# Rounds of two and of four experts in turn, one one-hot matrix ahead of the sort, and a branch hint, in a two-layer mixture-of-experts kernel

## The chip, the cores and the metric

The kernel runs on one core of a Trainium2 chip. The metric is device time in microseconds (us) of one launch; for the kernel before, the median of three runs is 997.89 us. Engines are PE (TensorE; PEld is its weight load), DVE (VectorE), ACT (ScalarE), POOL (GpSimd) and SP (SyncE, which here issues the loads of weights).

## The reference

256 tokens of width 1024 go through two layers and then a second block. Each layer is a mixer (a gated recurrence, a latent attention and a spatial gate), and then a sparse feed-forward part; only that part is touched here:

```python
for l in range(2):
    x = x + mixer(rms_norm(x))
    x = x + hier_moe(rms_norm(x))   # 32 experts, every token goes to 2 of them
x = second_block(x)

# hier_moe: the best of 4 groups, then the best 2 of its 8 experts; per expert, over its tokens:
h = silu(xi @ w1[e]) * (xi @ w3[e])   # 1024 -> 256
y = (h @ w2[e]) * weight              # 256 -> 1024
```

In float32 an expert's three matrices are 3 MB, so a layer reads 96 MB of expert weights.

## The kernel before

**Routing.** At the end of the mixer the tokens are scored (`Router`, from line 893). `slot` (line 994) says for each token and expert which place the token has in the expert's list. The eight experts 0 to 7 are static: they stand at places 0 to 7. The other 24 are sorted by the number of their tokens (lines 1000 to 1009, result `idm`) and stand at places 8 to 31; their number is known only then, and SP reads it into a register before it issues such a load (line 219). `perm` and `permb` hold the order as a matrix.

**Rounds.** `experts` works in 11 rounds. Places 0 to 11 go two at a time, with 64 tokens each (rounds 0 to 5, 6 MB of weights a round); places 12 to 31 go four at a time, with 32 tokens each (rounds 6 to 10, 12 MB a round). In either kind the array's 128 columns are full: the experts of a round stand side by side in it. A round does this:

- `onehot` (once for two rounds, on DVE, line 1093) makes the matrix P that picks the round's tokens; `gather` multiplies with it on PE (line 1127) and `gates` does the same for the gate weights (line 1106).
- `hidden` (line 1143) does the first product in two halves, one for each of an expert's first two weight chunks (c0, c1). In the middle of it `mid_way` runs: the second half of `combine` of the round before last, and `turn` of the round before. In round 1 `arrange` also runs there, which puts slots and weights into sorted order.
- `outp` (line 1179) does the second product, with the third chunk (c2), for the round before, and `combine` (line 1193) adds the result to the tokens. The gather for the next pair of rounds is woven into every second `outp`.

**Loads.** Every chunk is one DMA of 1 MB from SP's queue. The list `queue` fixes their order: for each round its c0, then its c1, then c2 of the round before. `pump` issues the next load when a buffer is free; `done` gives a buffer back, in the order of the program. In the expert stage 18 buffers are lent to the list: 5 of `w`, 6 of `a`, 1 each of `b`, `y` and `x`, 2 each of `hi` and `lo`. Loads of the last 8 places may not use `x`, `hi` and `lo` (`LATE`). Three chunks are loaded early, in the mixer, and the next layer's first chunk ("in") stands 8 loads ahead of the end.

**Overflow.** `most`, the highest number of tokens, is read into a register on every engine (line 1060). After the rounds, `tc.If(most > ...)` at line 1268 guards a long body for lists that are too long. With these inputs it is jumped over. `add_x` (line 395) then adds the sums to x on DVE, and the next mixer or the second block begins with transposes of x on PE (line 437).

`warm(n)` (line 386) issues n matmuls on constants, whose result nobody reads. The Tile framework orders the instructions of each engine by its own estimate of times, so instructions of neighbouring steps are interleaved.

Of the kernel before, what the change touches and what calls it, by code (L numbers as in the profile page):

```python
# [24 lines left out]
NE = 32  # L25


STATIC = 8
WIDE = 12
ROUNDS = [(64, list(range(i, i + 2))) for i in range(0, WIDE, 2)] + [(32, list(range(i, i + 4)))  # L30
                                                                    for i in range(WIDE, NE, 4)]
NR = len(ROUNDS)
SLOTS = 64
LATE = 8

N8 = dict(w=5, hi=2, lo=2, h=2, a=6, b=3, y=1, x=1)
N2 = dict(a=2, b=3, c=5)
# [68 lines left out]
def block_kernel(ctx: ExitStack, tc: tile.TileContext, A, out):  # L106
# [45 lines left out]
    def mm(tag):  # L152
        return pp.tile([128, 512], F32, name="mm", tag=f"ps_{tag}", bufs=NPS[tag])
# [10 lines left out]

    def late(key, tag):

        return tag in ("x", "hi", "lo") and key[2] >= NE - LATE

    def pump():

# [44 lines left out]
    def chunk_of(l, e, c):  # L215

        def ap():
            if e not in expert:
                expert[e] = nc.values_load(order[0][0:1, e - STATIC:e - STATIC + 1], engines=[SP], min_val=1,
                                           max_val=NE - STATIC)  # L220
            return A["w_e"][l, bass.ds(expert[e] + (STATIC - 1), 1), c].rearrange("e p n -> p (e n)")
        return (("e", l, e, c), A["w_e"][l, e, c] if e < STATIC else ap)

    for l in range(L):
        ex = []
        for i in range(NR + 1):
            for c in range(2):
                ex.extend(chunk_of(l, e, c) for e in (ROUNDS[i][1] if i < NR else ()))
            ex.extend(chunk_of(l, e, 2) for e in (ROUNDS[i - 1][1] if i else ()))
        for i in range(len(W_IN_CHUNKS)):  # L230
            a, b = W_IN_OFF[i], W_IN_OFF[i + 1]
            if l == 0 or i:
                queue.append((("in", l, i), A["w_in"][l][:, 8 * a:8 * b]))
            if i == 1:
                queue.append((("u", l), A["w_u"][l]))
            if i in EARLY:
                queue.append(ex.pop(0))
        queue.extend((("out", l, i), A["w_out"][l][:, i * 2048:(i + 1) * 2048]) for i in range(4))
        ex.insert(len(ex) - 8, following(l + 1))
        queue.extend(ex)  # L240
# [652 lines left out]
    class Router:  # L893
# [35 lines left out]
        def route(self):  # L929
# [44 lines left out]
            while chains:  # L974
                for c in list(chains):
                    try:
# [16 lines left out]
            slot = t1([128, 2, 32], "slot")  # L993
            nc.vector.scalar_tensor_tensor(slot, pr[:, :64].rearrange("p (j e) -> p j e", j=2), 1.0, ab,
                                           op0=OP.add, op1=OP.mult)

            nd = NE - STATIC
            k0, k1 = t1([128, nd], "key0"), t1([128, nd], "key1")
# [8 lines left out]
            idm = t1([128, nd], "idm", I32)  # L1007
            nc.vector.tensor_copy(idm, sk)
            nc.vector.tensor_scalar(idm, idm, 31, None, op0=OP.bitwise_and)
            perm = t1([NE, NE], "perm")  # L1010
            nc.vector.tensor_copy(perm[:, :STATIC], ident[:NE, :STATIC])
            nc.vector.tensor_scalar(perm[:, STATIC:], idm[:NE], float(STATIC), cc("place")[:NE], op0=OP.add,
                                    op1=OP.is_equal)
            permb = t1([NE, NE], "permb", BF)
            nc.vector.tensor_copy(permb, perm)

            mc, mci = t1([128, 3], "mc"), t1([1, 1], "mci", I32)
            nc.vector.tensor_reduce(mc[:, 0:1], pr[:, 64:64 + STATIC], AX, OP.max)
# [35 lines left out]
            rb_ = bc(rh, 2, NR)  # L1054
            nc.gpsimd.tensor_copy(whl[:, :, :, 0], rb_)
            nc.gpsimd.tensor_tensor(whl[:, :, :, 1], rb_, whl[:, :, :, 0].bitcast(F32), op=OP.subtract)
            weights_of(whl, wg, 0, STATIC)
            order[:] = [idm]
            expert.clear()
            most = nc.values_load(mci[0:1, 0:1], min_val=0, max_val=1 << 14)  # L1060
            lend("hi", N8["hi"])
            lend("lo", N8["lo"])
            lend("x", 1)
            return xh, xl, whl, slot, wg, (perm, permb, k0, sk), most

    def weights_of(whl, w, lo, hi):

        for a, b, n, i in ((lo, min(hi, WIDE), 2, lo // 2), (WIDE, hi, 4, WIDE // 2)):
            if a < b:
                m = (b - a) // n  # L1070
                for j in range(2):
                    v, o = w[:, j, a:b].rearrange("p (i e) -> p i e", e=n), whl[:, j, i:i + m]
                    nc.vector.tensor_copy(o[:, :, 2:2 + 2 * n:2], v)
                    nc.vector.tensor_sub(o[:, :, 3:2 + 2 * n:2], v, o[:, :, 2:2 + 2 * n:2].bitcast(F32))

    def experts(l, xh, xl, whl, slot, wg, perms, most):
# [5 lines left out]
        Ps, gts, hs = {}, {}, {}  # L1082
        X = big("h", [128, 8, 256], name="X")
        yhl = big("h", [128, 2, 2, 512], F32R, name="yhl")

        def onehot(q):

            rounds = ROUNDS[2 * q:2 * q + 2]
            n, places = rounds[0][0], sum((r[1] for r in rounds), [])
            P = Ps[q] = mid("c", [128, 2, 128 * len(rounds)], F32R, name="P")  # L1090
            by = slot if places[-1] < STATIC else slots[0]
            for j in range(2):
                nc.vector.tensor_tensor(P[:, j].rearrange("p (e s) -> p e s", e=len(places)),
                                        bc(cc("iota")[:, :n], 1, len(places)),
                                        bc(by[:, j, places[0]:places[-1] + 1], 2, n), op=OP.is_equal)

        def gates(q):

# [97 lines left out]
        def prepare_four(q, n):  # L1196
            if n:
                gates(q)
            gather(q, (2 * n, 2 * n + 1))

        onehot(0)
        prepare_four(0, 0)
        prepare_four(0, 1)

        slotT = small([NE, 2, 256], BF, name="slotT")
        slots = [None, slotT[:, 0], slotT[:, 1]]
# [5 lines left out]
        def arrange():  # L1212

            pt = mm("a")
            for j in range(2):
                nc.tensor.transpose(pt[:NE, j * 128:(j + 1) * 128], wg[:, j], ident)
            wgT = mid("b", [128, 256], name="wgT")[:NE]
            nc.scalar.activation(wgT, pt[:NE, :256], AF.Copy)
# [8 lines left out]
            nc.scalar.activation(slots[2], ps[:NE, :256], AF.Copy)  # L1227
            ps = mm("a")
            for j in range(2):
                nc.tensor.matmul(ps[:, j * NE:(j + 1) * NE], wgT[:, j * 128:(j + 1) * 128], perm, start=True, stop=True)  # L1230
            weights_of(whl, ps[:, :2 * NE].rearrange("p (j e) -> p j e", j=2), STATIC, NE)

        for i in range(NR):
            q, p = divmod(i, 2)
            last = 2 * q + 2 >= NR
            if i == NR - 2:
                x = big("x", [128, 2, D], name="x")
                for j in range(2):
                    nc.vector.tensor_add(x[:, j], xh[:, j].bitcast(F32), xl[:, j].bitcast(F32))

            def mid_way():
                if i > 1:
                    combine(i - 2, 1)
                if i:
                    turn(i - 1)
                if i == 1:
                    arrange()

            hidden(i, mid_way)
            if i == NR - 1:  # L1250
                reclaim()
                prepare(following(l + 1)[0])
            if p == 0 and not last:
                onehot(q + 1)
            if i:
                outp(i - 1, (lambda n: prepare_four(q + 1, n)) if p and not last else lambda n: None)
        combine(NR - 2, 1)
        turn(NR - 1)
        outp(NR - 1, lambda n: None)
        combine(NR - 1, 1)  # L1260
# [4 lines left out]
    def overflow(l, xh, xl, whl, slot, wg, key, sk, most):  # L1265

        g = vec[l][:, VC["ffn"]:VC["ffn"] + 8]
        with tc.If(most > SLOTS * 32 + 31):

            cap = mid("a", [128, NE], name="cap")  # L1270
            nc.vector.memset(cap, float(SLOTS))
# [410 lines left out]
```

## Time and profile before

| | before |
|---|---|
| median of 3 runs | 997.89 us (997.08 to 1001.84) |
| the profiled execution's own time | 1002.17 us |
| its span | 1000.4 us |
| mean granted TensorE clock | 0.979 |
| PE busy | 946.1 us (95%) |
| DVE, ACT busy | 473.6 us (47%), 378.8 us (38%) |
| DMA, mean | 273 GB/s |

Times in the rows count from the start of the span. The expert stage of the first layer runs from about 150 to 386 us, that of the second from about 532 to 765 us. PE's busy time includes matmuls that stand in the array at the same time, and its ends are modelled, so 95% says little by itself. The granted clock is a share of full speed: 1.00 is 2.4 GHz and 0.50 is 1.2 GHz.

### The profile page before, as it was taken

The page shows a single profiled execution, that of the slowest core. Times are in us where ns is not written, and L with a number is a line of the kernel's source. Part 1 is how long each engine was busy: PE and PEld are TensorE (multiplying, and loading weights), DVE is VectorE, ACT ScalarE, POOL GpSimd, SP SyncE. Part 2 cuts the span into 40 slices and gives each one's busy share as a digit, 9 for nine tenths or more (in the row PEclk, how much of TensorE's full clock was granted, in tenths as well). Part 3 has the DMA queues.
Part 4 walks back from the last instruction along what each step waited for, and adds up shares of the span by engine and source line. Part 5 has one row for each costly group of instructions (what it writes and reads, how often), then busy time and mean ns, then how long its engine had stood idle before and what let it go on. Part 6 is the DMA issues. An engine that isn't in the chain of part 4 may idle for free. (4 is left out here: it accounts for less than half of the span.)

```text
span 1000.4 us, 14950 instructions
## 1 busy us (share of the span) xinstructions
PE 946.1 (95%) x5818; PEld 624.5 (62%) x5820; DVE 473.6 (47%) x1149; ACT 378.8 (38%) x706; POOL 15.9 (2%) x56
## 2 busy tenths in 40 slices
PE   8999999999989887999999999999877999999998
PEld 6888874443433324989884434433323998899996
DVE  5798662221202213688664122212123776787574
ACT  6675532221211113485542221211111555755442
POOL 0100000000000001000000000000000000000000
PEclk9999997999999988999999999999998999999999
DMA  9538484898899996337566898999999443145431
GB/s 357 172 140 326 161 314 189 339 421 347 365 423 405 423 420 261 132 127 276 194 256 230 356 399 349 365 423 401 423 421 373 139 163 126 43 137 201 169 127 42
DMA packets 41438, 273.39 MB, mean 273 GB/s; under 512 B 5128, under 2 KB 7312, under 8 KB 9872
## 3 DMA queue, kind: packets, MB, share of 16 engines
q1 hardware_dynamic: 39008, 268.48, 68.3%
q10 hardware_dynamic: 2352, 3.87, 1.2%
q8 instruction: 49, 0.80, 0.3%
q14 instruction: 29, 0.24, 0.1%
HBM read 271.27 MB, written 2.63 MB: 274 GB/s over the span
## 5 line engine op out<-in xcount | busy, mean ns | idle before, releaser
L1143 PE MATMUL mm<-w,X 128*32 128x512 f32 (+1 forms) x1024 | 189.4, 611 | 8.8 <-DMA w<-in_w_e 8.8
L258 DVE TENSOR_TENSOR wlo<-w,whi 128x1024 fp32r<-128x1024 f32 (+3 forms) x124 | 144.1, 1173 | 29.0 <-ACT whi L257 28.9
L257 ACT ACTIVATE whi<-w 128x1024 fp32r<-128x1024 f32 (+3 forms) x124 | 122.4, 1016 | 75.8 <-issue 42.4
L1179 PE MATMUL mm<-w,ehT 128*32 128x512 f32 (+1 forms) x512 | 140.4, 607 | 4.5 <-DMA w<-in_w_e 2.4
L448 PE MATMUL mm<-hT,whi 128*128 128x256 f32 (+2 forms) x432 | 124.5, 289 | 0.3 <-ACT whi L257 0.3
L450 PE MATMUL mm<-hT,wlo 128*128 128x256 f32 (+2 forms) x432 | 123.8, 287 | 1.1 <-DVE wlo L258 1.1
L449 PE MATMUL mm<-lT,whi 128*128 128x256 f32 (+2 forms) x432 | 123.9, 287 | 0.0
L1143 PEld LDWEIGHTS mm<-w,X 128*32 128x32 f32 (+1 forms) x1024 | 48.3, 121 | 104.8 <-issue 82.9
L449 PE MATMUL mm<-wlo,hT 128*128 128x256 f32 x288 | 83.8, 291 | 1.1 <-DVE wlo L258 1.1
L448 PE MATMUL mm<-whi,hT 128*128 128x256 f32 x288 | 84.7, 294 | 0.0
L450 PE MATMUL mm<-whi,lT 128*128 128x256 f32 x288 | 83.7, 291 | 0.0
L448 PEld LDWEIGHTS mm<-hT,whi 128*128 128x128 f32 (+2 forms) x432 | 80.1, 186 | 2.2 <-ACT whi L257 0.6
L449 PEld LDWEIGHTS mm<-lT,whi 128*128 128x128 f32 (+2 forms) x432 | 80.0, 185 | 1.7 <-issue 1.3
L450 PEld LDWEIGHTS mm<-hT,wlo 128*128 128x128 f32 (+2 forms) x432 | 80.0, 185 | 1.8 <-DVE wlo L258 1.5
L1183 DVE TENSOR_TENSOR yhl<-mm,yhl 128x512 fp32r<-128x512 f32 x44 | 30.4, 691 | 106.6 <-ACT yhl L1182 105.6
L1130 ACT ACTIVATE X<-mm,vec 128x256 f32<-128x256 f32 (+1 forms) x96 | 43.5, 455 | 96.3 <-PE mm L1127 95.3
L1179 PEld LDWEIGHTS mm<-w,ehT 128*32 128x32 f32 (+1 forms) x512 | 32.3, 120 | 70.1 <-issue 53.2
L1151 DVE SCALAR_TENSOR_TENSOR eh<-eh,mm 128x256 f32<-128x256 f32 x22 | 9.3, 421 | 128.1 <-ACT eh L1150 128.1
L1127 PEld LDWEIGHTS mm<-P,xh 128*128 128x128 f32 x192 | 31.1, 200 | 54.7 <-ACT X L1130 34.5
L1150 ACT ACTIVATE eh<-mm,gt 128x256 f32<-128x256 f32 x22 | 10.4, 473 | 128.6 <-PE mm L1143 128.6
L449 PEld LDWEIGHTS mm<-wlo,hT 128*128 128x128 f32 x288 | 55.5, 193 | 2.8 <-DVE wlo L258 1.5
L1168 DVE TENSOR_SCALAR ePT<-mm,C 128x256 fp32r<-128x256 f32 x22 | 10.6, 483 | 97.8 <-ACT ehT L1166 97.8
(460 smaller groups left out, 1487.9 us busy)
## 6 DMA issues: line engine op xcount, KB each, us to landing
w<-in_w_e SPq DMA_DIRECT2D x192, 1024.0 KB, 8.8
w<-in_w_in SPq DMA_DIRECT2D x37, 1024.0 KB, 4.9
w<-in_w_out SPq DMA_DIRECT2D x12, 1024.0 KB, 5.0
w<-in_w_in SPq DMA_DIRECT2D x4, 768.0 KB, 6.1
w<-in_w_up_a SPq DMA_DIRECT2D x2, 1024.0 KB, 4.7
w<-in_w_up_b SPq DMA_DIRECT2D x2, 1024.0 KB, 4.8
w<-in_w_u SPq DMA_DIRECT2D x2, 960.0 KB, 14.7
w<-in_w_in SPq DMA_DIRECT2D x2, 800.0 KB, 8.6
```

What stands on the lines that cost most here:

```text
L257: nc.scalar.activation(hi[:, s_], w[:, s_], AF.Copy)
L258: nc.vector.tensor_sub(lo[:, s_], w[:, s_], hi[:, s_].bitcast(F32))
L448: nc.tensor.matmul(ps, st[0], mv[0], start=first, stop=False)
L449: nc.tensor.matmul(ps, st[0], mv[1], start=False, stop=False)
L450: nc.tensor.matmul(ps, st[1], mv[0], start=False, stop=last)
L1127: nc.tensor.matmul(ps[:, a, :n], t[:, j, k * 128:(k + 1) * 128], P[:, j], start=i == 0, stop=i == 3)
L1130: nc.scalar.activation(X[:, k, :n], ps[:, a, :n], AF.Identity, bias=0.0, scale=g[:, k:k + 1])
L1143: nc.tensor.matmul(ph[w * a:w * a + w], X[:, k, c0:c0 + w], take(kk_[a][k // 4])[:, (k % 4) * 512:(k % 4 + 1) * 512], start=k == 0, stop=k ...
L1150: nc.scalar.activation(h, ph[:, :256], AF.Tanh, scale=gts[q][:, p, 1:2])
L1168: nc.vector.tensor_scalar(PT, pT[:, 256:], cc("place" if w == 64 else "place32"), None, op0=OP.is_equal)
L1179: nc.tensor.matmul(py[w * a:w * a + w], hT[:, c * 128 + w * a:c * 128 + w * a + w], take(kk_[a][2])[:, c * 1024 + n * 512:c * 1024 + (n + ...
L1183: nc.vector.tensor_sub(yhl[:, n, 1], py, yhl[:, n, 0].bitcast(F32))
```

## The change

The order of the rounds becomes 2, 2, 4, 4, 2, 2, 4, 4, 2, 2, 4 experts, by places 0, 2, 12, 16, 4, 6, 20, 24, 8, 10, 28. The loads follow that order with one exception: the first two chunks of round 4 (places 4 and 5, static) come ahead of round 2's. `LATE` becomes the six places of the last two rounds. The first one-hot matrix is built right behind `slot`, ahead of the sort; `perm` and `permb` are built later. `arrange` is cut in two: the places in round 0, the weights in round 1, because round 2 now needs the sorted order. Three warming matmuls stand between the transposes of `slot` and the first gather. `most` is read into the registers just ahead of the last `turn` and no longer in the router, and there a branch hint for PE is set, behind a barrier that keeps the order of instructions and waits for nothing.

```diff
-ROUNDS = [(64, list(range(i, i + 2))) for i in range(0, WIDE, 2)] + [(32, list(range(i, i + 4)))
-                                                                    for i in range(WIDE, NE, 4)]
+ROUNDS = [(64, [a, a + 1]) if a < WIDE else (32, list(range(a, a + 4))) for a in (0, 2, 12, 16, 4, 6, 20, 24, 8, 10, 28)]
 NR = len(ROUNDS)
-LATE = 8
+LOADS = (0, 1, 4, 2, 3, 5, 6, 7, 8, 9, 10)
+LATE = [e for r in ROUNDS[-2:] for e in r[1]]
...
-        return tag in ("x", "hi", "lo") and key[2] >= NE - LATE
+        return tag in ("x", "hi", "lo") and key[2] in LATE
...
-        for i in range(NR + 1):
+        rounds = [ROUNDS[i][1] for i in LOADS]
+        for now, before in zip(rounds + [[]], [[]] + rounds):
             for c in range(2):
-                ex.extend(chunk_of(l, e, c) for e in (ROUNDS[i][1] if i < NR else ()))
-            ex.extend(chunk_of(l, e, 2) for e in (ROUNDS[i - 1][1] if i else ()))
+                ex.extend(chunk_of(l, e, c) for e in now)
+            ex.extend(chunk_of(l, e, 2) for e in before)
...
             nc.vector.scalar_tensor_tensor(slot, pr[:, :64].rearrange("p (j e) -> p j e", j=2), 1.0, ab,
                                            op0=OP.add, op1=OP.mult)
+            P = one_hot(0, slot)
...
-            most = nc.values_load(mci[0:1, 0:1], min_val=0, max_val=1 << 14)
...
-        onehot(0)
-        prepare_four(0, 0)
-        prepare_four(0, 1)
...
         nc.scalar.activation(slots[1], pt[:NE, :256], AF.Copy)
+        warm(3)
+        prepare_four(0, 0)
+        prepare_four(0, 1)
...
-                if i == 1:
-                    arrange()
+                (arrange_places, arrange_weights, lambda: None)[min(i, 2)]()
...
         combine(NR - 2, 1)
+        most = nc.values_load(mci[0:1, 0:1], min_val=0, max_val=1 << 14)
+        tc.no_sync_barrier()
+        tc.mark_branch_hint_location(f"fits{l}", hint=0, engines=[mybir.EngineType.PE])
         turn(NR - 1)
...
-        with tc.If(most > SLOTS * 32 + 31):
+        with tc.If(most > SLOTS * 32 + 31, label=f"fits{l}"):
```

`one_hot` holds the two instructions of the former `onehot`; `arrange_places` and `arrange_weights` hold those of `arrange`, and the weights of a pair of rounds are now split into high and low parts by two instructions for each pair.

## Rows read from the trace of the kernel before

**Rows 1.** The page's second part: GB/s in 40 slices of the span.
```profile
GB/s 357 172 140 326 161 314 189 339 421 347 365 423 405 423 420 261 132 127 276 194 256 230 356 399 349 365 423 401 423 421 373 139 163 126 43 137 201 169 127 42
```
**Rows 2.** First layer by stretch: us; PE, PEld, DVE, ACT, POOL busy; clock, DMA share, GB/s.
```profile
156.00:166.00 10.00, 10.00 (x38) 5.01 (x38) 0.55 (x4) 2.36 (x5) 0.00 (x0) 0.68 0.08 34
166.00:174.00 8.00, 8.00 (x39) 2.59 (x35) 0.90 (x2) 0.47 (x1) 0.00 (x0) 1.00 0.86 335
174.00:190.00 16.00, 16.00 (x73) 7.12 (x71) 4.63 (x18) 5.04 (x11) 0.00 (x0) 1.00 0.98 392
190.00:207.00 17.00, 17.00 (x79) 7.07 (x80) 3.43 (x7) 3.41 (x7) 0.00 (x0) 1.00 0.82 322
...
224.00:241.00 17.00, 17.00 (x78) 6.92 (x78) 3.43 (x7) 3.51 (x8) 0.00 (x0) 1.00 0.80 313
...
258.00:276.00 18.00, 18.00 (x112) 7.05 (x111) 3.59 (x8) 3.76 (x8) 0.00 (x0) 1.00 0.84 343
...
302.00:322.00 20.00, 19.11 (x137) 7.10 (x140) 4.35 (x9) 3.03 (x6) 0.00 (x0) 1.00 1.00 400
...
345.00:382.00 37.00, 32.70 (x160) 9.93 (x159) 8.13 (x11) 5.27 (x10) 0.00 (x0) 0.91 1.01 421
```
**Rows 3.** The same by stretch for the second layer's expert stage.
```profile
523.00:545.00 22.00, 20.07 (x107) 12.32 (x109) 13.12 (x89) 6.33 (x15) 0.99 (x4) 0.92 0.53 194
545.00:569.00 24.00, 24.00 (x109) 9.72 (x105) 5.53 (x20) 5.51 (x12) 0.00 (x0) 1.00 0.97 383
569.00:587.00 18.00, 18.00 (x83) 7.35 (x84) 3.43 (x7) 3.41 (x7) 0.00 (x0) 1.00 0.78 316
...
604.00:621.00 17.00, 17.00 (x80) 6.77 (x81) 3.43 (x7) 3.47 (x7) 0.00 (x0) 1.00 0.80 314
...
638.00:655.00 17.00, 17.00 (x110) 6.73 (x110) 3.43 (x7) 3.47 (x7) 0.00 (x0) 1.00 0.85 343
```
**Rows 4.** Who waited for whom on SP's queue, 140 to 345 us: total, times, longest.
```profile
SPq L1060 <- DVE cf L1042: 6.6, 1, 6.6
```
**Rows 5.** Instructions of PE in order of time: the first products of rounds 2 and 4.
```profile
189.21 0.64 PE L1143 MATMUL mm<-w,X 128*64 128x512 f32 x1
...
223.46 0.64 PE L1143 MATMUL mm<-w,X 128*64 128x512 f32 x1
```
**Rows 6.** Instructions of DVE in order of time, at slots and one-hot matrices, both layers.
```profile
149.98 0.23 DVE L994 SCALAR_TENSOR_TENSOR slot<-mm,ab 128x64 f32<-128x64 f32 x1
...
151.22 0.41 DVE L1093 TENSOR_TENSOR P<-C,slot 128x256 fp32r<-128x256 f32 x1
...
532.01 0.22 DVE L994 SCALAR_TENSOR_TENSOR slot<-mm,ab 128x64 f32<-128x64 f32 x1
```
**Rows 7.** Instructions of PE in order of time: warming, slot's transposes, the first gather.
```profile
144.56 4.98 PE L386 MATMUL mm<-ones_bf 128*128 128x512 bf16 x22
...
150.26 0.39 PE L1209 MATMUL mm<-C,slot 128*32 128x128 f32 x2 [0.32 <-DVE slot L994]
...
151.69 0.50 PE L1127 MATMUL mm<-P,xh 128*128 128x256 f32 x2 [1.03 <-DVE P L1093]
...
152.60 0.58 PE L1127 MATMUL mm<-P,xh 128*128 128x256 f32 x1 [0.42 <-DVE P L1093]
```
**Rows 8.** SP's loads in order of time: the first after the buffers were full, both layers.
```profile
165.80 0.34 SPq L184 DMA_DIRECT2D w<-in_w_e  x1
...
544.83 0.33 SPq L184 DMA_DIRECT2D w<-in_w_e  x1
```
**Rows 9.** All of line 1268 (the branch): min/median/max ns, first and last start.
```profile
L1268 DVEq COMPARE_BRANCH  x2: 63/68/72, 385.4 to 764.2; - x2
...
L1268 PEldq COMPARE_BRANCH  x2: 6202/6220/6239, 386.1 to 765.0; - x2
```
**Rows 10.** Instructions in order of time, DVE and PE, behind the branch.
```profile
386.20 2.48 DVE L395 TENSOR_TENSOR x<-x,mm 128x512 f32<-128x512 f32 x4 [0.71 <-PE mm L1193]
...
392.65 0.66 PE L437 MATMUL mm<-C,x 128*128 128x128 f32 x2 [6.37 <-PEq L1268]
```

More of the change, by code (lines that the diff above doesn't have):

```diff
@@ L29 @@
 WIDE = 12
-ROUNDS = [(64, list(range(i, i + 2))) for i in range(0, WIDE, 2)] + [(32, list(range(i, i + 4)))
-                                                                    for i in range(WIDE, NE, 4)]
+SLOTS = 64
+ROUNDS = [(64, [a, a + 1]) if a < WIDE else (32, list(range(a, a + 4))) for a in (0, 2, 12, 16, 4, 6, 20, 24, 8, 10, 28)]
 NR = len(ROUNDS)
-SLOTS = 64
-LATE = 8
+LOADS = (0, 1, 4, 2, 3, 5, 6, 7, 8, 9, 10)
+LATE = [e for r in ROUNDS[-2:] for e in r[1]]
 N8 = dict(w=5, hi=2, lo=2, h=2, a=6, b=3, y=1, x=1)
@@ L1009, in route @@
             nc.vector.tensor_scalar(idm, idm, 31, None, op0=OP.bitwise_and)
[L1010 to L1015, printed above, removed]
             mc, mci = t1([128, 3], "mc"), t1([1, 1], "mci", I32)
@@ L1056, in route @@
             nc.gpsimd.tensor_tensor(whl[:, :, :, 1], rb_, whl[:, :, :, 0].bitcast(F32), op=OP.subtract)
-            weights_of(whl, wg, 0, STATIC)
+            weights_of(whl, wg, 0)
+            perm = t1([NE, NE], "perm")
+            nc.vector.tensor_copy(perm[:, :STATIC], ident[:NE, :STATIC])
+            nc.vector.tensor_scalar(perm[:, STATIC:], idm[:NE], float(STATIC), cc("place")[:NE], op0=OP.add,
+                                    op1=OP.is_equal)
+            permb = t1([NE, NE], "permb", BF)
+            nc.vector.tensor_copy(permb, perm)
             order[:] = [idm]
             expert.clear()
-            most = nc.values_load(mci[0:1, 0:1], min_val=0, max_val=1 << 14)
             lend("hi", N8["hi"])
@@ L1063, in route, with weights_of, one_hot, experts @@
             lend("x", 1)
[L1064 to L1076, printed above, removed]
+            return xh, xl, whl, slot, wg, (perm, permb, k0, sk), P, mci
+    def weights_of(whl, w, *pairs):
+        for q in pairs:
+            rounds = ROUNDS[2 * q:2 * q + 2]
+            places = sum((r[1] for r in rounds), [])
+            n, m = len(rounds[0][1]), len(rounds)
+            v = w[:, :, places[0]:places[-1] + 1].rearrange("p j (i e) -> p j i e", e=n)
+            o = whl[:, :, 2 * q:2 * q + m]
+            nc.vector.tensor_copy(o[:, :, :, 2:2 + 2 * n:2], v)
+            nc.vector.tensor_sub(o[:, :, :, 3:2 + 2 * n:2], v, o[:, :, :, 2:2 + 2 * n:2].bitcast(F32))
+    def one_hot(q, by):
+        rounds = ROUNDS[2 * q:2 * q + 2]
+        n, places = rounds[0][0], sum((r[1] for r in rounds), [])
+        P = mid("c", [128, 2, 128 * len(rounds)], F32R, name="P")
+        for j in range(2):
+            nc.vector.tensor_tensor(P[:, j].rearrange("p (e s) -> p e s", e=len(places)),
+                                    bc(cc("iota")[:, :n], 1, len(places)),
+                                    bc(by[:, j, places[0]:places[-1] + 1], 2, n), op=OP.is_equal)
+        return P
+    def experts(l, xh, xl, whl, slot, wg, perms, P0, mci):
         nonlocal x
@@ L1081, in experts @@
         po = [[acc() for n in range(2)] for j in range(2)]
-        Ps, gts, hs = {}, {}, {}
+        Ps, gts, hs = {0: P0}, {}, {}
         X = big("h", [128, 8, 256], name="X")
@@ L1086, in onehot @@
         def onehot(q):
[L1088 to L1095, printed above, removed]
+            Ps[q] = one_hot(q, slot if ROUNDS[2 * q][1][0] < STATIC else slots[0])
         def gates(q):
@@ L1210, in experts, with arrange_places @@
         nc.scalar.activation(slots[1], pt[:NE, :256], AF.Copy)
[L1212 to L1218, printed above, removed]
+        warm(3)
+        prepare_four(0, 0)
+        prepare_four(0, 1)
+        def arrange_places():
             ps = mm("a")
@@ L1227, in arrange, with arrange_weights @@
             nc.scalar.activation(slots[2], ps[:NE, :256], AF.Copy)
+        def arrange_weights():
+            pt = mm("a")
+            for j in range(2):
+                nc.tensor.transpose(pt[:NE, j * 128:(j + 1) * 128], wg[:, j], ident)
+            wgT = mid("b", [128, 256], name="wgT")[:NE]
+            nc.scalar.activation(wgT, pt[:NE, :256], AF.Copy)
             ps = mm("a")
@@ L1230, in arrange @@
                 nc.tensor.matmul(ps[:, j * NE:(j + 1) * NE], wgT[:, j * 128:(j + 1) * 128], perm, start=True, stop=True)
-            weights_of(whl, ps[:, :2 * NE].rearrange("p (j e) -> p j e", j=2), STATIC, NE)
+            weights_of(whl, ps[:, :2 * NE].rearrange("p (j e) -> p j e", j=2), *range(1, (NR + 1) // 2))
         for i in range(NR):
```

## Prediction

> **What bounds the kernel now.** I read the page's GB/s slices first. They reach some 420 GB/s in the second half of either expert stage and no more [rows 1], so the question is whether the load queue or an engine sets the end there. The table by stretch answers it. From 345 to 382 us the DMA share is 1.01 at 421 GB/s, and PE is idle for 4 of 37 us; in the first half PE is busy throughout, and the queue runs at 313 to 392 GB/s in the stretches shown [rows 2]. So the first layer's stage goes from PE-bound to queue-bound. The second layer does the same [rows 3].
>
> The size of either limit: a 1 MB chunk at 421 GB/s takes 2.49 us. A round of two needs 6 chunks, 14.9 us of queue; a round of four needs 12, 29.9 us. PE needs 34.25 us from the first product of round 2 to that of round 4, so 17.1 us a round [rows 5]. A round of four has half the tokens per expert but fills the same columns, so I give it the same 17.1 us. Over a layer that is 11 x 17.1 = 188 us of PE against 96 x 2.49 = 239 us of queue. The queue is the limit of the stage as a whole, and what it stands idle is lost unless it is made up for by loads ahead. Only 18 buffers allow that.
>
> So I count the queue's idle time, stretch by stretch, as length x (1 - GB/s / 421). First layer: 1.6 us in 166-174, 1.1 in 174-190, 4.0 in 190-207, 4.4 in 224-241, 3.3 in 258-276, 1.0 in 302-322, together 15.4 [rows 2]. Second layer: 2.2 in 545-569, 4.5 in 569-587, 4.3 in 604-621, 3.2 in 638-655, together 14.2 [rows 3]. Before that comes a longer hole: all 18 buffers are full and the queue stands almost still (34 GB/s in 156-166) until the first round gives a buffer back and SP can issue again, at 165.80 and 544.83 us [rows 2, 8]. That moment is set by PE alone. Everything in a queue-bound stage is counted from it.
>
> **The order of the rounds.** I walk the loads through. The first 18 are in. Until the middle of round 2's first product the releases are as before: c0 and c1 of rounds 0 and 1 and c2 of round 0, ten buffers. Ten loads from 165.8 us end at 190.7, and round 2 starts at 189 and gives back its c0 some 6 us later. So the idle time of 166-207 stays: 6.7 us in the first layer. Then four chunks come back at once, about 195.5, four more after the second half at 200, two from round 1's `outp` at 205: ten loads, booked to 220. PE is at round 3's middle by about 212 and gives back four more. From there each round of four frees 12 buffers, 29.9 us of queue, in 17.1 us of PE: the queue has a free buffer waiting and PE waits for loads instead. Round 4 lies loaded already, so PE passes it and then waits for c2 of round 3. At that point, of the 18 buffers, 4 hold c0 and c1 of round 5, 2 hold c2 of round 4 and 4 are round 3's: ten. Eight are booked, some 20 us of queue. Rounds 4 and 5 then eat 2.2 us of this lead each (17.1 - 14.9), and rounds 6 and 7 build it up again. By this walk the queue does not stand still again.
>
> What goes is then 4.4 + 3.3 + 1.0 = 8.7 us in the first layer, and 4.3 + 3.2 = 7.5 in the second: **16.2 us**. Bounds: nothing, if the lead is eaten up elsewhere, and 15.4 + 14.2 = 29.6 us, if the early holes close as well. I take the walk. The second half of the old stage shows what hides PE's work in a queue-bound stretch: PE's own 17.1 us a round lies under 29.9 us of loads.
>
> **The one-hot matrix ahead of the sort, and the warming.** `slot` ends at 150.21, and the first instruction for P starts at 151.22 only, with the sort's instructions between [rows 6]. The gather starts at 151.69 and waits once more for P before 152.60; these waits are 1.03 and 0.42 us [rows 7]. Right behind `slot` the two instructions of 0.41 us end at about 150.6 and 151.0. The transposes end at 150.65. Three warming matmuls, at 4.98 / 22 = 0.23 us [rows 7], last to 151.33. So the gather starts 0.36 us earlier, and its third matmul some 0.9 us earlier, since P is whole by then: 0.9 us in each layer. Without the warming it would be 1.0 to 1.3, so the warming costs a little unless it holds the clock.
>
> The clock is the larger part. In 156-166 the granted clock is 0.68 in the first layer (6.4 of these 10 us at 1.2 GHz, the rest at 2.4); the second layer shows 0.92 over 523-545 [rows 2, 3]. PE stood idle just ahead, in the waits of [rows 7]. From `slot` to the first load issued again it is 165.80 - 149.98 = 15.8 us in the first layer and 544.83 - 532.01 = 12.8 in the second [rows 6, 8], for the same work: 3.0 us for the longer low clock. With the waits of 1.03 and 0.42 us filled I expect the first layer to be no worse than the second: 3.0 us. Sum: 2 x 0.9 + 3.0 = **4.8 us**. Bounds: a loss of 1.4 (warming for nothing, 2 x 0.7), and 2 x 1.3 + 3.0 + another 3.0 = 8.6, if neither layer loses any clock. It counts in full, because the queue stands still until that first release.
>
> **The branch.** The branch over the unused body takes 6.2 us on PE, 0.07 on DVE [rows 9]. DVE adds x behind it at 386.20 in four steps of 0.6 us; PE's first transposes come at 392.65, released by the branch alone [rows 10]. Without it they need the first step, 386.2 + 0.7 and a little for the signal, 387.1; the other half of the columns for the second pair comes 0.6 later. I take 5.4 us for each layer, **10.8 us**. PE would have time to fetch: behind the hint stands the wait for the last four chunks, 10.0 us of queue against 6.2. Bounds: nothing, and 2 x 6.2 = 12.4 and up to 3 us a layer for the clock behind the gap (the price found above).
> The Trainium skill (Runtime: NRT & Kernel Launch, Instruction fetch mechanics) says that a taken branch whose target lies outside the pages held makes the engine fetch that page first. The 6.2 us agree with it. The same section says that prefetch is purely sequential; by this a hint would fetch nothing, and the sum would lose this term. It is the first rival.
>
> **What I cost at nothing.** The register loads of `most`: SP's wait of 6.6 us for it in the router goes [rows 4], but what was queued behind it were loads into buffers that are full by 156 anyway. At the end they lie under PE's wait for the last chunks. Without that cover they would cost half a microsecond. The sorted places are needed two rounds earlier: SP's 17th and 18th loads now wait for `idm`, while nothing is released until 165.8, and `arrange_places` is three matmuls in round 0. If `idm` were late there, it would be late by the two one-hot instructions, 0.8 us, on queues with 10 us to spare. Two more small DVE instructions for the weights lie under PE. `LATE` opens five buffers to six more chunks, in a queue-bound stretch. The barrier binds the last `turn` behind all of round 9, 0.7 us of PE before loads that come later.
>
> **The sum.** 16.2 + 4.8 + 10.8 = 31.8 us. The profiled execution's span of 1000.4 becomes 968.6 us, its own time 1002.2 becomes 970.4. It was 4.3 us above the median of 997.9; from the median I get **966 us**. A change under 0.5%, 5 us, I count as no change.
>
> **Rivals.**
> - The hint does nothing. For it: nothing in this trace shows what a hint does. Against it: DVE's branch to the same place costs 0.07 us, so a branch is cheap where the target is at hand. 966 + 11 = 977 us. Chance 0.20. The rule of the Trainium skill cited above speaks for this rival.
> - The balance does not come: idle time moves into other stretches, because PE's order of instructions is fixed, and it waits for c2 of round 3 with round 5 loaded behind it. Then 966 + 16 = 982 us. Chance 0.12.
> - Slower: the buffers lock. Round 4's six chunks lie in 6 of the 18 buffers through rounds 2 and 3, and a round of four needs exactly the 12 that are left. If SP cannot run ahead, the queue stands still in each of rounds 2, 3, 6 and 7 while PE works. The gain of 16 us a layer is gone from 4 us of idle a round on; with 8 us a round the sum is 2 x 4 x 8 - 32 = 32 us slower, 1030 us. Against it: releases come chunk by chunk, in the order of the loads. Chance 0.08.
> - More than forecast: the early holes close too or no clock is lost, 945 to 953 us. Chance 0.06.
> - Two of the first failures together, with a small loss from the warming: 993 to 1000 us, no change. Chance 0.04.
>
> My forecast has 0.50. The range takes in the first two rivals and most of the bounds of the three terms: 952 to 986 us. The forecast's own range is 957 to 973. Faster: 0.50 + 0.20 + 0.12 + 0.06 = 0.88; same 0.04; slower 0.08.
>
> **What would show it.** The order: a DMA share of about 1 from round 2's middle to the end of the stage, with PE waiting for loads already in rounds 2 to 5, and the last expert chunk landing some 8 us sooner after the first release. The one-hot: P within 0.5 us of `slot`, the gather without its two waits, and the first release 12 to 13 us after `slot` in both layers. The branch: on PE well under 1 us, transposes 1 to 2 us after the first x is added. I am wrong if the queue shows new holes in rounds 2 and 3, if PE's branch still takes 6 us, or if the clock of the first gather stays low.

## The result, and the profile after

Medians: 968.44 us after (965.36 to 969.91, four runs) against 999.87 us before (997.08 to 1003.12, four runs). The ratio is 0.9684, 95% interval 0.9648 to 0.9719: 31.4 us less. The profiled execution after took 965.36 us with a span of 963.6, the fastest of its four; that of before was slower than its median. So the spans differ by more than the medians do, 36.8 us. Where those went, by stage, with starts read from the two traces (us; first layer, second layer):

| stretch | before | after | less by | forecast |
|---|---|---|---|---|
| `slot` to the first load issued again | 15.81, 12.82 | 10.75, 10.77 | 7.1 | 4.8 |
| that load to the end of the last `combine` | 220.48, 220.47 | 213.06, 212.56 | 15.3 | 16.2 |
| last `combine` to the first transpose of x | 6.37, 6.26 | 0.30, 0.30 | 12.0 | 10.8 |
| from there to the next `slot`, to the end | 139.36, 228.84 | 138.11, 227.93 | 2.2 | bound only |
| start to the first `slot` | 149.98 | 149.80 | 0.2 | 0 |

The load queue first. The GB/s slices of the page after, to be held against [rows 1]:

```profile
GB/s 357 180 131 324 203 249 248 362 417 421 421 421 421 420 417 306 94 171 273 199 251 253 355 416 420 422 420 421 421 420 330 181 159 99 45 175 178 186 118 44
```

The same by stretch, columns as in [rows 2]; the last two lines are of the second layer:

```profile
157.00:166.00 9.00, 9.00 (x47) 3.47 (x45) 1.13 (x4) 1.79 (x5) 0.00 (x0) 1.00 0.87 311
166.00:185.00 19.00, 19.00 (x87) 8.04 (x83) 5.71 (x23) 4.66 (x10) 0.00 (x0) 1.00 1.00 402
185.00:193.00 8.00, 8.00 (x63) 3.73 (x66) 0.36 (x1) 1.74 (x4) 0.00 (x0) 1.00 0.71 262
193.00:210.00 17.00, 15.56 (x100) 4.95 (x96) 3.55 (x8) 2.05 (x4) 0.00 (x0) 1.00 1.00 415
...
246.00:262.00 16.00, 16.00 (x68) 5.23 (x64) 3.46 (x6) 3.12 (x6) 0.00 (x0) 1.00 1.02 421
...
301.00:321.00 20.00, 17.85 (x86) 7.89 (x88) 2.82 (x9) 3.97 (x9) 0.00 (x0) 1.00 1.01 421
...
357.00:374.00 17.00, 16.21 (x103) 6.19 (x96) 5.72 (x10) 4.27 (x8) 0.00 (x0) 1.00 1.01 410
...
547.00:555.00 8.00, 8.00 (x59) 3.71 (x62) 0.13 (x1) 1.74 (x4) 0.00 (x0) 1.00 0.63 242
...
571.00:700.00 129.00, 126.36 (x620) 47.70 (x613) 20.32 (x50) 23.66 (x48) 0.00 (x0) 0.99 1.01 421
```

The dips to 347 and 365 between the slices of 421 are gone. One larger hole is left in each layer behind the first release, 185 to 193 and 547 to 555, and after it the queue runs at its limit to the end. The clock is 1.00 where [rows 2] show 0.68.

DVE and PE in order of time (start, us, engine, line), around `slot` and behind the last round:

```profile
149.80 0.23 DVE L996 SCALAR_TENSOR_TENSOR slot<-mm,ab 128x64 f32<-128x64 f32 x1
...
150.06 0.76 DVE L1085 TENSOR_TENSOR P<-C,slot 128x256 fp32r<-128x256 f32 x2
...
373.03 2.48 DVE L397 TENSOR_TENSOR x<-x,mm 128x512 f32<-128x512 f32 x4 [0.21 <-PE mm L1199]
```

```profile
150.54 0.51 PE L1133 MATMUL mm<-P,xh 128*128 128x256 f32 x2
150.94 0.81 PE L388 MATMUL mm<-ones_bf 128*128 128x512 bf16 x3
151.40 0.47 PE L1133 MATMUL mm<-P,xh 128*128 128x256 f32 x1
...
360.76 3.71 PE L1185 MATMUL mm<-w,ehT 128*64 128x512 f32 x16
364.39 2.30 PE L1199 MATMUL mm<-yhl,ePT 128*128 128x512 f32 x8
366.63 0.43 PE L1165 MATMUL mm<-C,eh 128*128 128x128 f32 x2
366.99 0.29 PE L1169 MATMUL mm<-slotT,bf_ident 32*32 32x256 bf16 x4
367.76 3.64 PE L1185 MATMUL mm<-w,ehT 128*32 128x512 f32 x32 [0.49 <-ACT ehT L1172]
371.33 2.28 PE L1199 MATMUL mm<-yhl,ePT 128*128 128x512 f32 x8
373.91 0.90 PE L439 MATMUL mm<-C,x 128*128 128x128 f32 x4 [0.30 <-DVE x L397]
```

P is built right behind `slot`, and the gather no longer waits for it (two waits in [rows 7]). PE runs the three warming matmuls behind the gather's first two, not ahead of them. PE's transposes begin 0.88 us after DVE's first step at x, where [rows 10] had 6.45, and they now wait for x, not for the branch. Behind the first gap the kernel before ran at the lower clock, the kernel after does not (one line of each, columns as in [rows 2]):

```profile
391.00:398.00 7.00, 5.35 (x24) 5.06 (x25) 3.69 (x7) 5.00 (x15) 3.89 (x16) 0.51 0.04 14
...
374.00:390.00 16.00, 15.68 (x123) 14.60 (x124) 11.52 (x27) 10.64 (x24) 5.71 (x19) 1.00 0.39 136
```

The last `outp`, at 367.76, shows no wait for a load; this is taken up under the experiments.

The branch (columns as in [rows 9]), and SP's first load after the buffers were full (as [rows 8]):

```profile
L1279 PEldq COMPARE_BRANCH  x2: 438/460/481, 372.9 to 734.6; - x2
```
```profile
160.56 0.33 SPq L185 DMA_DIRECT2D w<-in_w_e  x1
...
522.79 0.33 SPq L185 DMA_DIRECT2D w<-in_w_e  x1
```

On PE it falls from 6.22 us to 0.46. The next fence lists who waited for whom on SP's queue from 140 to 345 us. SP's wait for the register load (L1266, the former L1060 of [rows 4]) has not gone: 7.4 us, where it was 6.6. The load now stands behind round 9 in the source, but SP still runs it at 152 us.

```profile
SPq L1266 <- DVE cf L1038: 7.4, 1, 7.4
```

### The profile page after: what moved, and what is told of

It reads as the page before. It is cut to its first block, busy times and chain, and to the rows that moved or that the text cites. A ratio compares the mean times of both kernels' runs of the same rounds, so it can differ in the third digit from the quotient of the medians.

```text
span 963.6 us, 14970 instructions
## 1 busy us (share of the span) xinstructions
PE 937.1 (97%) x5826; PEld 615.8 (64%) x5826; DVE 474.4 (49%) x1149; ACT 377.3 (39%) x706; POOL 15.9 (2%) x56
## 4 chain that ended last, share of the span: by engine, by line
PE 85%; DVE 6%; ACT 5%; DMA 3%; issue 1%; SPq 0%; DVEq 0%; ACTq 0%
PE mm L1149 18%; PE mm L1185 12%; PE mm L450 11%; PE mm L451 11%; PE mm L452 11%; PE mm L1133 6%; PE mm L1199 5%; DMA w<-in_w_e 3%; DVE wlo L260 1%; PE mm L562 1%; ACT whi L259 1%; PE mm L1165 1%; PE mm L567 1%; ACT X L1136 1%; PE mm L680 1%
## 5 line engine op out<-in xcount | busy, mean ns | idle before, releaser
L1185 PE MATMUL mm<-w,ehT 128*32 128x512 f32 (+1 forms) x512 | 134.9, 603 | 1.0 <-ACT ehT L1172 1.0
L1185 PEld LDWEIGHTS mm<-w,ehT 128*32 128x32 f32 (+1 forms) x512 | 31.8, 119 | 66.6 <-issue 59.6
L450 PEld LDWEIGHTS mm<-whi,hT 128*128 128x128 f32 x288 | 55.0, 191 | 1.6 <-issue 0.9
```

What stands on the lines that cost most here:

```text
L450: nc.tensor.matmul(ps, st[0], mv[0], start=first, stop=False)
L1185: nc.tensor.matmul(py[w * a:w * a + w], hT[:, c * 128 + w * a:c * 128 + w * a + w], take(kk_[a][2])[:, c * 1024 + n * 512:c * 1024 + (n + ...
```

## The experiments

Spans hold one execution each, and the first `slot`, ahead of any edit, lies between 149.8 and 154.6 us in them. So the profiles are compared by the first four stretches of the table above, called *release*, *rounds*, *gap* and *mixer* in that order.

**The parts by themselves.** Three kernels hold one part each. The order of rounds and loads alone is the changed kernel less these lines, with P and `perm` built where they were and the register load of `most` back in the router:

```diff
-            P = one_hot(0, slot)
...
-        warm(3)
...
-        tc.no_sync_barrier()
-        tc.mark_branch_hint_location(f"fits{l}", hint=0, engines=[mybir.EngineType.PE])
```


> The kernel before with the new order of rounds and loads alone (the cut of arrange and LATE with it), no early one-hot, no warming, no hint. Theory: the terms add up, so the stretch from the first release to the last combine goes from 220.5 us to about 213 in each layer, the first release stays 15.8 and 12.8 us behind slot, PE's branch stays at 6.2 us, and the whole gains 15 to 16 us (ratio about 0.985). Rival: the rounds became shorter because they start earlier and at full clock, not because of their order; then that stretch stays above 218 us and the whole gains less than 5 us.

Measured: 989.62 us, ratio 0.9889 (0.9841 to 0.9938), so 11 us. Rounds 214.77 and 215.98, releases 11.69 and 12.85, gaps 4.76 and 6.34. The queue did all that it does in the changed kernel; the rounds did not (more on that below).

The hint alone, in the kernel before:

```diff
-            most = nc.values_load(mci[0:1, 0:1], min_val=0, max_val=1 << 14)
...
+        most = nc.values_load(mci[0:1, 0:1], min_val=0, max_val=1 << 14)
+        tc.no_sync_barrier()
+        tc.mark_branch_hint_location(f"fits{l}", hint=0, engines=[mybir.EngineType.PE])
         turn(NR - 1)
...
-        with tc.If(most > SLOTS * 32 + 31):
+        with tc.If(most > SLOTS * 32 + 31, label=f"fits{l}"):
```


> The kernel before with the branch hint alone (register load of most, barrier, hint and label). Theory: PE's branch falls from 6.2 to about 0.5 us, the gap from the last combine to the first transposes from 6.4 to 0.3 us in both layers, and 1 to 2 us more behind it because the clock does not fall there: 13 to 14 us (ratio about 0.986). Rival: the mixer behind the branch then waits for its own first weights, so that half of it is given back: 6 to 7 us.

Measured: 984.0 us, ratio 0.9841 (0.9786 to 0.9896), 16 us. Gaps 0.30 and 0.30, rounds 219.21 and 219.93, mixer 138.17 against 139.36. By the two profiles the gaps give 12.0 us and the mixer 2.1. The releases, ahead of the hint, are 12.75 and 11.47, 4.4 us shorter than before: the low clock behind `slot` lasts less long in this execution. The rounds give 1.8 more.

The one-hot matrix ahead of the sort with the warming, in the kernel before:

```diff
+            P0 = mid("c", [128, 2, 256], F32R, name="P")
+            for j in range(2):
+                nc.vector.tensor_tensor(P0[:, j].rearrange("p (e s) -> p e s", e=4), bc(cc("iota")[:, :64], 1, 4),
+                                        bc(slot[:, j, 0:4], 2, 64), op=OP.is_equal)
...
-        onehot(0)
...
+        warm(3)
```


> The kernel before with the early one-hot matrix and the three warming matmuls alone (perm built later, as in the change). Theory: from slot to the first load issued again it takes about 10.8 us in both layers instead of 15.8 and 12.8, with the granted clock at 1.0 there, and the rest of the stage keeps its 220.5 us, as the queue sets its end: 7 us (ratio 0.993). Rival: in the old order the first six rounds are bound by PE and the last five by loads, so the early start only gives the queue a longer hole: the stretch behind the first release grows and less than 2 us are left.

Measured: 994.9 us, ratio 0.9937 (0.9915 to 0.996), 6.3 us. Releases 10.74 and 10.74, rounds 220.01 and 219.79. The three parts sum to 11.1 + 15.9 + 6.3 = 33.3 us, against 31.4 together: within what these intervals allow, they add up. By stretch the profiles do not. The releases shrink by 4.1, 4.4 and 7.1 us in the three kernels and by 7.1 in the changed one, though only the third builds P early; the rounds shrink by 10.2, 1.8 and 1.2 us, together 13.2, against 15.3.

**The exception in the order of the loads.** Round 4's chunks are loaded when their turn comes:

```diff
-LOADS = (0, 1, 4, 2, 3, 5, 6, 7, 8, 9, 10)
+LOADS = (0, 1, 2, 3, 4, 5, 6, 7, 8, 9, 10)
```


> The changed kernel with the loads in the order of the rounds, that is without the exception for round 4's first chunks. Theory: the exception keeps SP from needing sorted places while the queue is still filling, and spares the queue about 2 us a layer by my walk through the loads; without it the changed kernel is 3 to 5 us slower (stretch behind the first release 215 instead of 213 us). Rival: round 4's chunks only take 6 of 18 buffers away from rounds 2 and 3; without the exception PE waits less there and the kernel is as fast or 2 to 4 us faster.

Measured: 981.76 us, ratio 0.9804 (0.9755 to 0.9852); 12 us of the 31 are lost, three times what was expected. By stretch, and SP's longest wait:

```profile
141.00:157.00 16.00, 15.50 (x97) 10.72 (x97) 12.98 (x72) 5.63 (x15) 0.99 (x4) 1.00 0.00 1
157.00:165.00 8.00, 7.79 (x44) 4.50 (x44) 2.73 (x19) 3.57 (x8) 0.00 (x0) 1.00 0.66 240
```
```profile
SPq L1266 <- DVE cf L1038: 28.0, 1, 28.0
```

The queue stands still through 141 to 157, at 1 GB/s, where a second profile of the changed kernel, with its `slot` at the same 154 us, has 253. Only ten chunks have a place that is known without the sort. The eleventh needs the sorted order, and SP waits for the end of the sort with eight buffers empty: the register load of `most` (L1266) stands ahead of that of the place, and the first load goes out at 158.40. The exception is what keeps the queue fed across the sort. From `slot` to the last `combine` it takes 232.5 and 230.5 us instead of 223.8 and 223.3; this profiled execution is the slowest of its six.

**The hint late, and none.** In one kernel the barrier and the hint stand right ahead of the second half of the last `combine`; in the other the hint's value is 1 instead of 0:

```diff
-        tc.no_sync_barrier()
-        tc.mark_branch_hint_location(f"fits{l}", hint=0, engines=[mybir.EngineType.PE])
         turn(NR - 1)
         outp(NR - 1, lambda n: None)
+        tc.no_sync_barrier()
+        tc.mark_branch_hint_location(f"fits{l}", hint=0, engines=[mybir.EngineType.PE])
         combine(NR - 1, 1)
```


> The changed kernel with barrier and hint moved down to just ahead of the last half of the last combine, some 1 to 2 us ahead of PE's branch. Theory: the hint starts a fetch that takes as long as the branch did without it, about 6 us, so a hint 1 to 2 us ahead leaves 4 to 5 us in the branch and the gap to the first transposes is 4 to 5 us again. Rival: the hint only tells the sequencer which way to go and needs no time ahead; then the branch stays at 0.5 us and the gap at 0.3.

```diff
-        tc.mark_branch_hint_location(f"fits{l}", hint=0, engines=[mybir.EngineType.PE])
+        tc.mark_branch_hint_location(f"fits{l}", hint=1, engines=[mybir.EngineType.PE])
```


> The changed kernel with the hint's value 1 in place of 0, which names the other way, into the body that isn't run. Theory: the wrong way is fetched, so PE's branch costs at least what it cost without a hint, 6 us or more, and the gap at both layers' ends is 6 us or more: about 12 us slower than the changed kernel. Rival: what helps is the barrier and the register load moved ahead, not the hint; then the branch stays under 1 us.

One execution each: 984.75 and 981.46 us. The branch in the kernel with the late hint, and in the one with the value 1:

```profile
L1279 PEldq COMPARE_BRANCH  x2: 5016/5988/6959, 377.8 to 747.2; - x2
```
```profile
L1279 PEldq COMPARE_BRANCH  x2: 6057/6076/6096, 376.6 to 744.8; - x2
```

The hint in the changed kernel, the same columns:

```profile
L1689 PEldq BRANCH_PREFETCH_HINT  x2: 36/40/45, 366.5 to 728.2; - x2
```

With 0.29 and 0.46 us between hint and branch, 5.0 and 7.0 us are left, which is no gain: in the four kernels without a hint the branch takes 4.6 to 6.5 us. In the changed kernel PE executes the hint at 366.53 and 728.25 and the branch 6.3 us later, and 0.48 and 0.44 are left. So the hint starts something that needs more than 0.5 us and is done after 6.3, beside the matmuls; no run has a lead between the two. With the value 1 the trace holds no hint instruction at all. So this kernel does not show what a hint of the wrong way costs; it is the control with the barrier and the moved register load but no hint, and its gaps are 5.64 and 5.68 us. The hint alone closes the gap.

**Without the warming.**

```diff
-        warm(3)
```


> The changed kernel without the three warming matmuls. Theory: the early one-hot alone fills most of the waits, so the clock holds in most executions and the first load comes some 0.4 us sooner behind slot (10.3 us instead of 10.75): no change that can be measured, within 1 us. Rival: the warming is what holds the clock; without it the granted clock falls to 0.5 for 3.4 us or more behind slot and the first load comes after 12 us or more in one or both layers, 2 to 6 us slower.

Measured: 967.32 us, ratio 0.967 (0.9617 to 0.9723). Releases 10.14 and 10.14, no stretch of low clock behind `slot`. The warming costs 0.6 us of the release in each layer, and in these executions it holds nothing that the early P does not hold by itself. At the end of the stage the 0.6 us do not show: from `slot` to the last `combine` it is 224.7 and 223.2 us, against 223.8 and 223.3.

Releases over all profiles: 10.74 to 10.77 us in the 14 layers of the seven profiles with early P, warming, 18 buffers and a queue that is full before the sort; 10.14 in the four layers with early P and no warming; 15.81, 12.82, 11.69, 12.85, 12.75 and 11.47 in the six layers with P behind the sort. The two shortest of these six show no low clock there. So a clean layer takes 11.6; the stretches of 10.2 us at half the clock cost 4.2 and those of 3.4 us 1.2. Early P with the warming is worth 0.8 to 0.9 against a clean layer, and 1.4 without the warming. The clock fell in four of six layers with P behind the sort, and in one of 22 with early P (the first layer with 13 buffers, below). That is a count; why it falls in some and not in others is open.

**Fewer buffers: the rival on the slower side.** The changed kernel with 13 buffers for expert chunks instead of 18:

```diff
-            lend("hi", N8["hi"])
-            lend("lo", N8["lo"])
-            lend("x", 1)
```


> The changed kernel with 13 buffers in place of 18 (hi, lo and x aren't lent to the loads). Theory: the loads only need some buffer free, in order; five fewer chunks are in when the queue first stands still, 5 x 2.49 = 12.4 us a layer, and from then on the queue runs as before: some 25 us slower than the changed kernel. Rival: with round 4's six chunks held through rounds 2 and 3 the buffers lock, so the queue stands still in every round of four as well: 40 us or more slower, with holes in the GB/s behind the first release.

Measured: 1023.36 us, ratio 1.0246 (1.0193 to 1.03). By stretch:

```profile
196.00:206.00 10.00, 9.95 (x47) 2.78 (x48) 1.84 (x4) 1.18 (x2) 0.00 (x0) 1.00 0.42 155
206.00:240.00 34.00, 25.26 (x127) 7.00 (x125) 2.98 (x6) 2.29 (x6) 0.00 (x0) 0.95 1.00 413
240.00:256.00 16.00, 16.00 (x71) 6.14 (x70) 1.94 (x6) 3.20 (x7) 0.00 (x0) 1.00 0.59 231
```

That is the lock: at 0.42 of the queue PE is busy and all buffers wait for it, then PE stands idle for 9 of 34 us until the chunks arrive, and again. The rounds take 238.08 and 236.85 us, 24.7 a layer more. The five chunks that can't be loaded ahead explain 5 x 2.49 = 12.4 of them. The queue's standstill in the first and the third line is 10 x (1 - 155 / 421) = 6.3 and 16 x (1 - 231 / 421) = 7.2 us, where the changed kernel has the 3.0 of 185 to 193: some 10 us more, and most of the rest. The mechanism of the rival is real, and 18 buffers are enough to keep it away.

**What sets the end of the stage.** In the changed kernel nothing waits for the last chunk. From the packets in the trace, the last expert chunk lands 203.7 and 203.5 us after the first release (212.9 and 212.8 before), yet the last `combine` ends 9.3 and 9.0 us after that landing, where it was 7.6 and 7.7. Two kernels move the next mixer's first weight behind the last expert chunks, one of them without warming:

```diff
-        ex.insert(len(ex) - 8, following(l + 1))
+        ex.append(following(l + 1))
...
-                prepare(following(l + 1)[0])
...
         combine(NR - 1, 1)
+        prepare(following(l + 1)[0])
```


> The changed kernel with the next stage's first chunk behind all expert loads of the layer instead of 8 loads ahead of the end, and its split moved behind the last combine. Theory: the queue sets the end of the stage, so the last expert chunk lands one load, 2.5 us, sooner and the stage from slot to the last combine is 221 instead of 223.5 us in both layers; the chunk lands about when the last combine ends and its split (two times 1.05 us on ACT) lies beside the additions to x: 3 to 5 us in all (ratio to the changed kernel 0.995 to 0.997). Rival: the split then comes late for the first products of the next mixer, so that what the rounds gain the gap behind them loses: no change, within 1 us.

> The same without the three warming matmuls. Theory: both act by themselves, another 0.6 us a layer from the earlier first release: 1 us less than the run above, if the clock holds. Rival: the clock falls behind slot in some executions and the times scatter more, up to 5 us longer.

Measured: 971.47 us, ratio 0.971 (0.9679 to 0.9741), and 970.0 us, 0.9681 (0.965 to 0.9712). In the first of them the last chunk lands 202.1 and 200.7 us after the release, 1.7 and 2.8 us sooner than in the changed kernel, and the rounds take 214.31 and 212.68, no less. In the second it lands after 201.7 and 201.3, and the rounds take 213.8 and 213.9. The expected gain of 3 to 5 us does not come: an earlier chunk brings nothing. The next kernel takes work from PE instead, and a plain copy of the changed kernel runs beside it:

```diff
-                    for t in (xh, xl):
+                    parts = (xh, xl) if q < 2 else (xh,)
+                    for t in parts:
...
-                                             stop=i == 3)
+                                             stop=i == 2 * len(parts) - 1)
```


> The changed kernel, whose gathers for rounds 4 to 10 leave out the product with the low part of x (xl), so its output loses that part: about 7 us a layer less work for PE, from round 3 on; no load is changed, and the first release and the early holes of the queue come before it. Theory, PE sets the end of the stage: in the changed kernel the last expert chunk lands 203.6 us after the first release and the last combine ends 9.3 us later, of which some 6 us (the last outp of 3.6 us and its combine of 2.3 us) have to follow the landing. So the time from first release to the end of the last combine falls from 213 us to about 210, by at most 3.5 us a layer, the landing stays at 203 to 204, and with 2 x 3 us the median is some 6 us below that of the changed kernel, 961 to 964 us. Rival, the queue sets the end by way of the releases: landing and end stay where they are, 203.6 and 213 us, 967 to 969 us. A third case: PE's shorter work gives buffers back sooner, and landing and end both come sooner.

> The changed kernel as it is, beside the kernel with less work for PE on the same chip: 966 to 970 us, 213 us from first release to last combine in both layers, as in its first profile.

Measured: 964.96 us, ratio 0.9648 (0.9615 to 0.9682), beside 969.14, 0.9682 (0.9653 to 0.971). Landing at 203.7 in both layers, rounds 211.01 and 211.02, against 211.80 and 212.60 in the copy and 213.06 and 212.56 in the first profile. The last `outp` of the kernel with less work, and its chain of waits:

```profile
364.87 1.25 PE L1186 MATMUL mm<-w,ehT 128*32 128x512 f32 x6 [0.49 <-ACT ehT L1173]
367.56 3.62 PE L1186 MATMUL mm<-w,ehT 128*32 128x512 f32 x26 [1.45 <-DMA w<-in_w_e]
```
```profile
354.52 13.00 DMA w<-in_w_e
```

Now PE waits for the last load in the last round. The theory holds, PE sets the end in the changed kernel, with a size of 0.8 to 2 us a layer rather than the 3.5 at most: where PE does wait for the last load, the stage ends 7.3 us behind its landing, at 211.0. The intervals of the two medians, 4.2 us apart, overlap; the landings and the waits carry the verdict.

**A gain that was put down to nothing: the barrier.** The kernel with the order alone has the same landings, 203.6 and 203.8 us, but ends 11.2 and 12.2 us after them. PE's instructions at its end:

```profile
361.35 1.93 PE L1185 MATMUL mm<-w,ehT 128*64 128x512 f32 x4
363.21 0.44 PE L1165 MATMUL mm<-C,eh 128*128 128x128 f32 x2
363.58 0.29 PE L1169 MATMUL mm<-slotT,bf_ident 32*32 32x256 bf16 x4
363.80 3.65 PE L1185 MATMUL mm<-w,ehT 128*64 128x512 f32 x12
367.38 1.66 PE L1199 MATMUL mm<-yhl,ePT 128*128 128x512 f32 x6
368.97 1.04 PE L1185 MATMUL mm<-w,ehT 128*32 128x512 f32 x2
369.95 0.73 PE L1199 MATMUL mm<-yhl,ePT 128*128 128x512 f32 x2
370.61 3.67 PE L1185 MATMUL mm<-w,ehT 128*32 128x512 f32 x30
```

The same work as in the changed kernel from 360.76 on, in another order. There `outp` of round 9 is one piece of 16 in 3.71 us and that of round 10 one of 32 in 3.64; here they fall into 4 and 12, and 2 and 30, with transposes and `combine` between. The counts are matmuls in the trace, two for each product in the source. In a whole piece of round 10 four of them, for different columns, start within 0.02 us of each other and the next four 0.43 us later; alone, each takes 0.45 to 0.59 us. So the small pieces take 1.93 and 1.04 us. From the start of that `outp` to the end of the last `combine` it is 15.1 us instead of 12.9. The kernel with the late hint, whose barrier stands later too, has the same cut order, and rounds of 216.35 and 215.29; the kernel with the value 1 has the barrier in its place, no hint, whole pieces, and rounds of 212.12 and 212.72. The pieces are whole as well in the copy and in the kernel without the warming, whose rounds are 214.5 and 213.1. So it is the barrier ahead of the last `turn`, not the hint, that shortens the rounds: 215.6 us on the average of the four layers without it, 212.8 of the eight with it, 2.8 us a layer. No run takes the barrier alone out of the changed kernel.

PE is cut up in the same way in the middle of the changed kernel, rounds 3 and 4:

```profile
213.80 1.04 PE L1185 MATMUL mm<-w,ehT 128*32 128x512 f32 x2
...
215.44 1.07 PE L1149 MATMUL mm<-w,X 128*64 128x512 f32 x2
216.45 1.04 PE L1185 MATMUL mm<-w,ehT 128*32 128x512 f32 x2
...
228.56 3.62 PE L1185 MATMUL mm<-w,ehT 128*32 128x512 f32 x20
```

Two matmuls take 1.04 us there, twenty 3.62. From the first product of round 4 to that of round 6 it takes 25.7 + 26.8 us, where two rounds before took 34.25 [rows 5]. This was not undone in any run; whether an order with whole pieces there would bring the end nearer to 211.0 stays open.

## Why the prediction was right, and where it was not

- **The order of the rounds** was forecast at 16.2 us and the stretch gave 15.3, but not as the walk had it. The queue's part came out larger: the last chunk lands 9.1 and 9.3 us sooner after the release, where 8.7 and 7.5 were forecast. That it then does not stand still again held from 193 us on, and in the second layer from 555. The step that failed is "PE waits for loads instead": behind its wait of 1.4 us at 209 PE hardly waits for a load, and the queue no longer sets the end. The walk gave PE 17.1 us for every round; in the new order rounds 4 and 5 take 25.7 and 26.8, so PE is busy to the end of the stage. The order alone gives 5.7 and 4.5 us in the rounds. The remaining 5.1 come, by the comparisons above (2.8 us a layer), from the barrier, which the prediction had put down as 0.7 us of PE's work ahead of later loads. The term's size came out right by luck: an omitted gain filled an omitted loss.
- **The one-hot matrix** was forecast at 4.8 us, of it 1.8 for the earlier start and 3.0 for the clock; it gave 7.1. The start was right (0.8 to 0.9 a layer). The clock term was too small: it took the second layer as the undisturbed one, and that layer lost 1.2 us itself; against a clean layer the first lost 4.2. The upper bound had this. It also hangs on the execution: the six layers with P behind the sort take 12.9 us on average, and against that the two layers gain 4.3, near the forecast. The warming, which the prediction called a little costly unless it holds the clock, costs 0.6 us of the release in a layer.
- **The branch** was forecast at 10.8 us; the gaps gave 12.0. PE is through the branch before DVE has x, so all but 0.30 us of the gap goes. Behind it the stretches of low clock at 391 and 770 us (0.51 over 7 us in both) went too and gave 2.2 us more, which stood in the bounds only. The first rival, an inert hint, is refuted by the kernel with the value 1. The Trainium skill (Runtime: NRT & Kernel Launch, Instruction fetch mechanics) calls prefetch purely sequential; here the same branch costs 6.06 and 6.10 us without the hint and 0.44 and 0.48 with it 6.3 us ahead, and the measurement decides.
- **At nothing.** "SP's wait goes" was wrong: 6.6 us became 7.4, for the load is still read at 152 us. It cost nothing for the reason given, full buffers. Moving the sorted places cost nothing that shows; but for the exception in the order of the loads it would have, by 12 us.
- **The rivals.** The lock of the buffers happens at 13 and not at 18. The balance did come in the queue; that PE's fixed order would eat part of it, as that rival had it, is true for 8 us of the order alone (landing 9.2 and 9.0 us sooner, end 5.7 and 4.5), and the barrier brings most of them back.
- **The sum** was 31.8 us against one execution and 966 us from the median. By spans it was 36.8, by medians 31.4: the two profiled executions lay on opposite sides of their medians, by 2.3 and 3.1 us.

## What to carry to other kernels

When a stage stops being bound by its load queue, look at once at what ends it next: here the chunks came 9 us sooner, and PE's order of instructions decided how much of that arrived at the end. Narrow matmuls that overlap side by side are worth keeping in one piece, and a barrier that fixes order and waits for nothing can do that. A branch hint needs room ahead of the branch: 6.3 us, about what the branch costs without it, were enough, half a microsecond brought nothing, and what lies between was not measured.

## What the runs showed of the hardware

- A hint for the branch takes 5.6 us of 6.1 from PE with 6.3 us of lead. With 0.3 to 0.5 us of lead the branch takes 5.0 and 7.0 us, about as in the eight layers without a hint (4.6 to 6.5).
- Two column-tiled matmuls of 32 columns alone take 1.04 us; 32 of them in one piece, four side by side, take 3.64.
- One queue held 421 GB/s on this core over 129 us (571 to 700).
- A 10.2 us stretch at the lower of the two clocks cost 4.2 us against layers without one (11.6), less than the half of it that the clock alone would take.
